# First-layer roots by way of device memory: a row of reciprocal roots goes over the partitions through a small array and two transfers, not through TensorE

## The chip, the cores and the metric

The kernel runs on one core of one Trainium2 chip. The metric is device time in microseconds of one execution. A core has TensorE (PE, matmuls; PEld its weight loads), VectorE (DVE), ScalarE (ACT), GpSimd (POOL) and SyncE (SP), each with its own instruction queue, worked in order, and 16 DMA engines that all of the queues share.

## The reference

Two layers over x (256 rows, 1024 columns, float32), then a last RMSNorm. One layer, cut to what matters:

```
def rms_norm(x, gain):
    xf = xf * lax.rsqrt(jnp.mean(xf * xf, axis=-1, keepdims=True) + EPS)
    return xf * gain

hn = rms_norm(x, norm_gain)
proj = jnp.einsum('bsd,de->bse', hn, w_in)
a_q, a_k, a_v, a_g, b_x, b_g, c_q, c_k, c_v, c_g = jnp.split(proj, ...)
y_a = dilated_attention(rope(a_q), rope(a_k), a_v) * silu(a_g)
y_b = rg_lru_branch(b_x, ...) * silu(b_g)
y_c = stick_breaking_attention(c_q, c_k, c_v) * silu(c_g)
return x + concat([y_a, y_b, y_c]) @ w_out
```

Only the factor `rsqrt(mean(x*x) + EPS)`, one number for each of the 256 rows of x, is touched by the change, and only in the first layer.

## The kernel before

Everything is in one program, `trunk_kernel`. Weights come as chunks of 128 x 2048 float32 (`w_pack`, two transfers of 512 KB each, issued by SyncE into five staging buffers `st`). To keep float32 accuracy each chunk is split in two: ScalarE rounds a quarter of it to the matmul's format (`whi`, line 109), VectorE subtracts that from the original (`wlo`, line 110), four of each a chunk. A product is then three matmuls: high by high, high by low, low by high (`mm3`, line 212). A staging buffer is free for the next transfer when VectorE has subtracted its second half.

**First layer.** Here the projections start from x itself (already transposed and multiplied by the gain, lines 142 to 171), without the normalising factor. Because that factor is one number for each row of x, it can be multiplied in later, on the results. `rms_stats` (line 191) makes it for each of the two blocks of 128 rows: ScalarE squares and sums, VectorE adds (line 196), ScalarE takes the logarithm and an exponential (`rstd`, lines 198 and 200). The result is a column: 128 partitions, one number each.

Results with rows of x on the partitions (`va`, `vc`, lines 385 and 386) take that column directly. Results that are kept transposed (heads on the partitions, rows of x along the free dimension) need the same 256 numbers as a row, repeated on all 128 partitions: the tile `rb`, 128 x 256. `rows_of_rstd` (line 373) makes it: VectorE scales the identity matrix by the column (line 377), TensorE multiplies a matrix of ones with it (line 378; a float32 matmul runs as two passes here, four in all), VectorE copies the result out of PSUM (line 379).

`rb` is then read by VectorE alone: in `scaled` (line 391) for `qc` and `kc`, the queries and keys of stick-breaking attention, and later for `bxp` and the gates; for `rp0`, the rotation tables multiplied by it (line 612); and in `rotated` (line 490).

**Order of the work.** TensorE's order is the order in which the program is written (a manual schedule for this engine). Around the change it is: chunk CQ (two halves of 128 outputs), chunk CK first half, `rows_of_rstd` (given to `proj_b` as `mid`, run between the two halves), CK second half, chunk AQ0 first half, the stick-breaking scores (line 442, which read `qc` and `kc`), AQ0 second half, AK0, BX and so on. On the other engines the framework's scheduler sets the order when the program is built; on the chip each engine then works through its list strictly. GpSimd has little to do: a polynomial of 4 columns, some memsets, and two transfers within SBUF, `xs` (line 565).

Of the kernel before, what the change touches and what calls it, by code (L numbers as in the profile page):

```python
# [9 lines left out]
F32 = mybir.dt.float32  # L10
# [3 lines left out]
ALU = mybir.AluOpType  # L14

P = 128
S = 256
D = 1024
L = 2
NT = S // P  # L20
# [22 lines left out]
CH_AV, CH_CV, CH_CQ, CH_CK, CH_BX, CH_CG, CH_BG, CH_AG, CH_O = 0, 2, 3, 4, 7, 10, 11, 12, 14  # L43
# [5 lines left out]
def trunk_kernel(ctx: ExitStack, tc: tile.TileContext, x, first_x, first, wpack, prm_d, gatew, gains, consts, rope, out):  # L49
    nc = tc.nc  # L50
    act, dve, pe, gps = nc.scalar, nc.vector, nc.tensor, nc.gpsimd

    cst = ctx.enter_context(tc.tile_pool(name="cst", bufs=1))
# [3 lines left out]
    wk = ctx.enter_context(tc.tile_pool(name="wk", bufs=2))  # L57
    pp = ctx.enter_context(tc.tile_pool(name="pp", bufs=3, space=bass.MemoryType.PSUM))
    at = ctx.enter_context(tc.tile_pool(name="at", bufs=4, space=bass.MemoryType.PSUM))
    yp = ctx.enter_context(tc.tile_pool(name="yp", bufs=1, space=bass.MemoryType.PSUM))  # L60

    def bank(pool, tag):
        return pool.tile([P, 512], F32, name=tag, tag=tag)

    def scr(w):
        return wk.tile([P, 512], F32, name="scr", tag="scr", bufs=SCR)[:, 0:w]
# [15 lines left out]
    def tab(*a, **k):  # L82
        i = dep(act.activation(*a, **k), loaded["load"])  # L83
        loaded["users"].append(i)
        return i

    def v2(a, n=2):
        return a.rearrange("p (b t) -> p b t", b=n)
# [28 lines left out]
    def ask(l, c, ahead=AHEAD):  # L117
        last = order.index((l, c)) + ahead
        while pending and order.index(pending[0]) <= last:
            i = pending.pop(0)  # L120
            ready[i] = load_chunk(*i)

    def weights(l, c, ahead=AHEAD):
        ask(l, c, ahead)
        return ready.pop((l, c))
# [16 lines left out]
    for k in range(NK):  # L142
# [7 lines left out]
        o = k % 2 * 768  # L150
# [16 lines left out]
        for (i, (a, b)), (ps, base, c0, c1) in seq:  # L167
            for t in range(NT):
                pe.matmul(ps[t][:, c0 - base:c1 - base], a[:, k, t * P:(t + 1) * P], b[:, c0:c1],  # L169
                          start=k == 0 and i == 0 and c0 == base, stop=k == NK - 1 and i == 2,  # L170
# [9 lines left out]
    ident = con[:, C_ID:C_ID + P]  # L180
# [4 lines left out]
    tiny_t = cst.tile([P, 48], F32, name="tiny")  # L185
    tiny = tiny_t[:, 0:1]
    dve.memset(tiny, 1e-19)
    ones = cst.tile([P, P], F32, name="ones")
    dve.memset(ones, 1.0)

    def rms_stats(t, eng):
        sq = wk.tile([P, 2], F32, name="sq", tag="sq", bufs=2)
        for i in range(2):
            act.activation(scr(512), xres[:, t, i * 512:(i + 1) * 512], AF.Square, accum_out=sq[:, i:i + 1])
        ss = wk.tile([P, 1], F32, name="ss", tag="ss", bufs=2)
        eng.tensor_scalar(ss, sq[:, 0:1], 1.0 / D, EPS, ALU.mult, ALU.add)
        ln = wk.tile([P, 1], F32, name="lnv", tag="lnv", bufs=2)
        tab(ln, sq[:, 1:2], AF.Ln, bias=ss, scale=1.0 / D)
        rstd = wk.tile([P, 1], F32, name="rstd", tag="rstd", bufs=4)
        tab(rstd, ln, AF.Exp, scale=-0.5)  # L200
        return rstd

# [4 lines left out]
    def mm3(ps, lhs, rhs, ks, first, last):  # L207
        lh, ll = lhs
        rh, rl = rhs
        seq = [(a, b, k) for a, b in ((lh, rh), (lh, rl), (ll, rh)) for k in ks]  # L210
        for i, (a, b, k) in enumerate(seq):
            pe.matmul(ps, a(k), b(k), start=first and i == 0, stop=last and i == len(seq) - 1)  # L212
# [33 lines left out]
    def normed(t):  # L246
        rstd = rms_stats(t, gps)
        xns = []
        for half in range(2):
            xn = scr(512)  # L250
            cs = slice(half * 512, half * 512 + 512)
            dve.scalar_tensor_tensor(xn, xres[:, t, cs], rstd, gn[:, cs], ALU.mult, ALU.mult)
            xns.append(xn)
        return xns
# [40 lines left out]
    rb = cst.tile([P, S], F32, name="rb")  # L295
    gn = cst.tile([P, D], F32, name="gn", tag="gn")

    for l in range(L):
# [14 lines left out]
        def proj_b(c, mid=None, to=None, sc=1.0):  # L313
            pair = c in PAIRED[l]
            hi, lo = [a.rearrange("p (k c) -> p k c", c=256) for a in weights(l, c, AHEAD - 1 if mid else AHEAD)]
            if pair:
                flat = None if to is not None else scr(512)
                to = [v2(flat)[:, b, :] for b in range(2)] if to is None else to
            else:
                flat = bank(pp, "pp")  # L320
            for b in range(2):
                cs = slice(b * P, b * P + P)
                if pair:
                    ps = bank(pp, "pp")
                    seq = [(0, k) for k in range(NK - 1)] + [(1, k) for k in range(NK)] + [(0, NK - 1)]
                    for i, (is_lo, k) in enumerate(seq):
                        if is_lo:
                            pe.matmul(ps[:, 0:S], lo[:, k, cs], xh[:, k, :], start=False, stop=False,  # L328
                                      skip_group_check=True)
                        else:  # L330
                            pe.matmul(ps, hi[:, k, cs], xx[:, k].rearrange("p h t -> p (h t)"), start=i == 0,  # L331
                                      stop=i == len(seq) - 1, skip_group_check=True)
                    low = wk.tile([P, S], F32, name="low", tag="low", bufs=2)
                    act.activation(low, ps[:, S:2 * S], AF.Copy, scale=sc)  # L334
                    if sc == 1.0:
                        dve.tensor_add(to[b], ps[:, 0:S], low)
                    else:
                        dve.scalar_tensor_tensor(to[b], ps[:, 0:S], sc, low, ALU.mult, ALU.add)
                else:
                    mm3(flat[:, b * 256:(b + 1) * 256], [lambda k, a=a: a[:, k, cs] for a in (hi, lo)],  # L340
                        [lambda k, a=a: a[:, k, :] for a in (xh, xl)], range(NK), True, True)
                if b == 0 and mid:
                    mid()
                    ask(l, c)
            return flat

        def proj_to(dst, c, mid=None, sc=1.0):
            if l > 0 and c in PAIRED[l]:
                proj_b(c, mid, [dst[:, b, :] for b in range(2)], sc)
            else:  # L350
                scaled(dst, proj_b(c, mid), sc)
# [16 lines left out]
            cv_bk = [cv_ps[:, t * 256:(t + 1) * 256] for t in range(NT)]  # L368

        if l == 0:  # L370
            rstd0 = [rms_stats(t, dve) for t in range(NT)]

        def rows_of_rstd():
            rb_ps = bank(yp, "y")
            for t in range(NT):
                dg = scr(P)
                dve.tensor_scalar(dg, ident, rstd0[t], None, ALU.mult)
                pe.matmul(rb_ps[:, t * P:(t + 1) * P], ones, dg, start=True, stop=True)
            dve.tensor_copy(rb, rb_ps[:, 0:S])

        va = sb.tile([P, NT, 512], F32, name="va", tag="va")
        vc = sb.tile([P, NT, 256], F32, name="vc", tag="vc")
# [5 lines left out]
        def scaled(dst, ps, sc=1.0):  # L388
            if l == 0:
                a, b = rows(ps)  # L390
                dve.scalar_tensor_tensor(dst, a, sc, b, ALU.mult, ALU.mult)
            else:
                act.activation(dst, v2(ps), AF.Copy, scale=sc)
# [208 lines left out]
        else:  # L602
            cq_ps = proj_b(CH_CQ)
        if l == 0:
            ck_ps = proj_b(CH_CK, rows_of_rstd)
            scaled(qc, cq_ps, 0.125)
            scaled(kc, ck_ps)
        else:
            proj_to(kc, CH_CK)
# [189 lines left out]
```

## Time and profile before

| | |
|---|---|
| median of 3 runs | 248.68 us (248.48 to 250.25) |
| the profiled execution's own time | 248.61 us |
| its span in the profile | 246.5 us |
| granted TensorE clock, mean | 0.995 |
| TensorE busy | 238.6 us |
| VectorE busy | 193.3 us |
| ScalarE busy | 170.5 us |
| GpSimd busy | 11.3 us |

The page of the profile gives busy time for each engine, the chain of work that ended last, and groups of instructions by line. Times of the timeline are microseconds from the span's start; a row has start, duration, engine, line, operation, `out<-in`, shape, count, and in brackets how long the engine was idle before it and what ended that. Consecutive instructions of one kind are one row.

### The profile page before, as it was taken

What the parts mean: (1) busy time and instruction counts of PE and PEld (TensorE: products, weight loads), DVE (VectorE), ACT (ScalarE), POOL (GpSimd) and SP (SyncE); (2) the same over time, 40 slices, a digit from 0 to 9 for tenths busy, and PEclk for the clock granted to TensorE, in tenths of its full rate; (3) what the DMA queues carried; (4) which work ended last, traced back from release to release, by engine and by line L of the source; (5) the groups of instructions that cost most, each with busy time, mean ns of one, the idle gap of its engine ahead of it and who ended that gap; (6) DMA issues with size and microseconds to landing.
All of it is one profiled execution on the core that took longest, in us unless ns stands there. A gap on an engine that the chain in (4) does not pass through costs nothing.

```text
span 246.5 us, 4741 instructions
## 1 busy us (share of the span) xinstructions
PE 238.6 (97%) x1753; PEld 212.4 (86%) x1753; DVE 193.3 (78%) x454; ACT 170.5 (69%) x368; POOL 11.3 (5%) x45
## 2 busy tenths in 40 slices
PE   7999999999999999999999999999999999999990
PEld 4889999999998899878889988888889889987870
DVE  3875599999999789986693666999999967985253
ACT  3867989854688499974672775876589749992142
POOL 0027100000100000000000000000010000000000
PEclk9999999999999999999999999999999999999997
DMA  6999799377737632277258387506462752000022
GB/s 208 390 289 412 313 316 322 112 237 255 229 102 233 231 96 78 89 237 251 108 166 256 101 297 256 201 6 204 148 205 56 233 228 85 3 0 0 3 85 85
DMA packets 13174, 43.90 MB, mean 178 GB/s; under 512 B 1632, under 2 KB 2144, under 8 KB 13152
## 3 DMA queue, kind: packets, MB, share of 16 engines
q1 hardware_dynamic: 12384, 42.30, 50.9%
q10 hardware_dynamic: 576, 0.79, 0.9%
q0 software_dynamic: 192, 0.52, 0.8%
q8 instruction: 14, 0.23, 0.3%
q14 instruction: 8, 0.07, 0.1%
HBM read 42.03 MB, written 1.05 MB: 175 GB/s over the span
## 4 chain that ended last, share of the span: by engine, by line
PE 94%; DMA 2%; DVE 1%; ACT 1%; SPq 0%; issue 0%; ACTq 0%
PE pp L212 51%; PE pp L331 11%; PE s L212 9%; PE pp L328 5%; PE s L169 4%; PE s L462 3%; PE s L514 2%; PE y L426 2%; DMA st<-first 2%; PE pp L169 2%; PE s L442 1%; PE pp L426 1%; PE s L573 1%; PE s L260 1%; DVE xres L689 0%; ACT scr L243 0%
## 5 line engine op out<-in xcount | busy, mean ns | idle before, releaser
L110 DVE TENSOR_TENSOR wlo<-st,whi 128x512 fp32r<-128x512 f32 x132 | 84.0, 684 | 12.6 <-ACT whi L109 12.3
L109 ACT ACTIVATE whi<-st 128x512 fp32r<-128x512 f32 x132 | 73.8, 628 | 20.2 <-DMA st<-w_pack 7.5
L212 PE MATMUL pp<-xx,whi 128*128 128x256 f32 x480 | 63.8, 285 | 0.0
L212 PEld LDWEIGHTS pp<-xx,whi 128*128 128x128 f32 x480 | 59.7, 191 | 1.3 <-ACT whi L109 0.4
L212 PE MATMUL pp<-xx,wlo 128*128 128x256 f32 x240 | 33.7, 283 | 0.0
L212 PEld LDWEIGHTS pp<-xx,wlo 128*128 128x128 f32 x240 | 31.0, 192 | 0.0
L331 PE MATMUL pp<-xx,whi 128*128 128x512 f32 x112 | 29.2, 396 | 0.0
L331 PEld LDWEIGHTS pp<-xx,whi 128*128 128x128 f32 x112 | 20.1, 189 | 3.9 <-ACT scr L83 0.3
L83 ACT ACTIVATE pr<-scr,mn 128x128 f32<-128x128 f32 (+1 forms) x32 | 14.1, 442 | 8.4 <-DVE mn L521 8.4
L77 ACT ACT_TABLE_LOAD x13 | 16.7, 1283 | 1.9 <-PEq L792 1.7
L328 PEld LDWEIGHTS pp<-xx,wlo 128*128 128x128 f32 x112 | 15.3, 190 | 1.1
L328 PE MATMUL pp<-xx,wlo 128*128 128x256 f32 x112 | 15.6, 282 | 0.0
L212 PE MATMUL pp<-whi,yh 128*128 128x512 f32 x48 | 14.4, 400 | 0.0
L212 PE MATMUL pp<-wlo,yh 128*128 128x512 f32 x48 | 13.8, 390 | 0.0
L212 PE MATMUL pp<-whi,yl 128*128 128x512 f32 x48 | 13.8, 389 | 0.0
L212 PEld LDWEIGHTS pp<-wlo,yh 128*128 128x128 f32 x48 | 9.0, 188 | 1.9
L212 PEld LDWEIGHTS pp<-whi,yl 128*128 128x128 f32 x48 | 9.0, 188 | 1.9
L212 PEld LDWEIGHTS pp<-whi,yh 128*128 128x128 f32 x48 | 8.6, 188 | 1.9 <-issue 0.3
L414 ACT ACTIVATE yh<-scr 128x512 fp32r<-128x512 f32 x8 | 5.1, 631 | 7.3 <-DVE scr L412 7.2
L169 PE MATMUL s<-whi,xx 128*128 128x512 f32 (+1 forms) x36 | 9.6, 384 | 0.2
L521 DVE CUSTOM_DVE_ANT_0 scr<-s,con 128x128 f32<-128x128 f32 (+1 forms) x32 | 9.2, 351 | 0.0
L334 ACT ACTIVATE low<-pp 128x256 f32<-128x256 f32 x14 | 5.3, 376 | 5.1 <-PE pp L331 5.1
(175 smaller groups left out, 357.4 us busy)
## 6 DMA issues: line engine op xcount, KB each, us to landing
st<-w_pack SPq DMA_DIRECT2D x66, 512.0 KB, 5.0
st<-first SPq DMA_DIRECT2D x7, 512.0 KB, 5.7
xres<-x_in SPq DMA_DIRECT2D x2, 512.0 KB, 8.7
gw_t<-gate_w SPq DMA_DIRECT2D x2, 256.0 KB, 7.7
gn<-gains SPq DMA_DIRECT2D x1, 512.0 KB, 6.2
xs<-xc POOLq DMA_DIRECT2D x4, 128.0 KB, 4.8
gf<-gains SPq DMA_DIRECT2D x1, 512.0 KB, 6.8
out<-scr SPq DMA_DIRECT2D x2, 256.0 KB, 2.1
```

What stands on the lines that cost most here:

```text
L77: load = act.preload_act_table_set(name)
L83: i = dep(act.activation(*a, **k), loaded["load"])
L109: split[l, c] = act.activation(hi[:, ws], st[:, ss], AF.Copy)
L110: dve.tensor_sub(lo[:, ws], st[:, ss], hi[:, ws].bitcast(F32))
L169: pe.matmul(ps[t][:, c0 - base:c1 - base], a[:, k, t * P:(t + 1) * P], b[:, c0:c1], start=k == 0 and i == 0 and c0 == base, stop=k == NK - ...
L212: pe.matmul(ps, a(k), b(k), start=first and i == 0, stop=last and i == len(seq) - 1)
L328: pe.matmul(ps[:, 0:S], lo[:, k, cs], xh[:, k, :], start=False, stop=False, skip_group_check=True)
L331: pe.matmul(ps, hi[:, k, cs], xx[:, k].rearrange("p h t -> p (h t)"), start=i == 0, stop=i == len(seq) - 1, skip_group_check=True)
L334: act.activation(low, ps[:, S:2 * S], AF.Copy, scale=sc)
L426: pe.matmul(y[hr, p * 128 + o:p * 128 + 256], vt[:, s0, hs], wts[i][s0], start=s0 == 0, stop=s0 == 1)
L462: pe.transpose(tp[:, i * P:(i + 1) * P], tiles[h0 + h][:, j * P:(j + 1) * P], ident)
L521: dve.tensor_tensor_reduce(xs[:, cs], sps[h][:, cs], nmask[:, cs], -0.125, 3e38, ALU.add, ALU.min, mn[:, t:t + 1])
```

## The change

`rms_stats` may now write its result into a given column. The two columns of the first layer lie side by side in a spare part of the tile `tiny` (`both`, 128 x 2). ScalarE issues a transfer that stores them, transposed, into an array `rd` of 2 x 128 float32 in device memory; GpSimd issues a transfer that loads these 256 numbers as one row, repeated, into all 128 partitions of `rb`. `rows_of_rstd`, its two scalings, its matmuls, its copy and the matrix of ones are gone, and `proj_b(CH_CK)` has no `mid` any more.

```
+    dr = ctx.enter_context(tc.tile_pool(name="dr", bufs=1, space=bass.MemoryType.DRAM))
...
-    ones = cst.tile([P, P], F32, name="ones")
-    dve.memset(ones, 1.0)
-
-    def rms_stats(t, eng):
+    def rms_stats(t, eng, rstd=None):
...
-        rstd = wk.tile([P, 1], F32, name="rstd", tag="rstd", bufs=4)
+        rstd = wk.tile([P, 1], F32, name="rstd", tag="rstd", bufs=4) if rstd is None else rstd
...
-            rstd0 = [rms_stats(t, dve) for t in range(NT)]
-
-        def rows_of_rstd():
-            rb_ps = bank(yp, "y")
-            for t in range(NT):
-                dg = scr(P)
-                dve.tensor_scalar(dg, ident, rstd0[t], None, ALU.mult)
-                pe.matmul(rb_ps[:, t * P:(t + 1) * P], ones, dg, start=True, stop=True)
-            dve.tensor_copy(rb, rb_ps[:, 0:S])
+            both = tiny_t[:, 32:32 + NT]
+            rstd0 = [rms_stats(t, dve, both[:, t:t + 1]) for t in range(NT)]
+            rd = dr.tile([NT, P], F32, name="rd")
+            act.dma_start(out=rd.rearrange("t p -> p t"), in_=both)
+            gps.dma_start(out=rb, in_=rd.rearrange("(o t) p -> o (t p)", o=1).broadcast_to([P, S]))
...
-            ck_ps = proj_b(CH_CK, rows_of_rstd)
+            ck_ps = proj_b(CH_CK)
```

Because VectorE's and ScalarE's lists are made by the scheduler, the change moves more than it names. The number behind a tile's name is its buffer; names in brackets are what the row waits for. VectorE before, from the last subtraction of chunk CK (`wlo_374`) through AQ0 (`wlo_388`) and AK0 (`wlo_484`) to `kc` (the two scalings of the identity stand some rows ahead of this piece):

```order
L110 TENSOR_TENSOR wlo_374<-st_381,whi_373 128x512 [waits Activation_49]
L110 TENSOR_TENSOR wlo_388<-st_389,whi_387 128x512 [waits DVE_49,DMAHW5_49,PE_49,Activation_49]
L110 TENSOR_TENSOR wlo_388<-st_389,whi_387 128x512 [waits Activation_49]
L110 TENSOR_TENSOR wlo_388<-st_395,whi_387 128x512 [waits DMAHW6_49,Activation_49]
L110 TENSOR_TENSOR wlo_388<-st_395,whi_387 128x512 [waits Activation_49]
L379 COPY rb_293<-y_475 128x256 [waits PE_49]
L110 TENSOR_TENSOR wlo_484<-st_485,whi_483 128x512 [waits DMAHW7_49,DVE_49,Activation_49]
L110 TENSOR_TENSOR wlo_484<-st_485,whi_483 128x512 [waits Activation_49]
L391 SCALAR_TENSOR_TENSOR qc_326<-pp_401,rb_293 128x512 [waits DVE_49]
L110 TENSOR_TENSOR wlo_484<-st_491,whi_483 128x512 [waits DMAHW0_49,Activation_49]
L110 TENSOR_TENSOR wlo_484<-st_491,whi_483 128x512 [waits Activation_49]
L391 SCALAR_TENSOR_TENSOR kc_327<-pp_450,rb_293 128x512 [waits PE_49]
```

VectorE after the change, the same place, from the last subtraction of CK (`wlo_375`) through AQ0 (`wlo_389`) to the first half of AK0 (`wlo_452`) and `kc`:

```order
L111 TENSOR_TENSOR wlo_375<-st_382,whi_374 128x512 [waits Activation_49]
L386 SCALAR_TENSOR_TENSOR qc_327<-pp_402,rb_293 128x512 [waits DMASW0_49,PE_49]
L111 TENSOR_TENSOR wlo_389<-st_390,whi_388 128x512 [waits DMAHW6_49,DVE_49,Activation_49]
L111 TENSOR_TENSOR wlo_389<-st_390,whi_388 128x512 [waits Activation_49]
L607 TENSOR_TENSOR rp0_292<-rp_291,rb_293 128x256 [waits DMAHW1_49]
L111 TENSOR_TENSOR wlo_389<-st_396,whi_388 128x512 [waits DMAHW7_49,Activation_49]
L111 TENSOR_TENSOR wlo_389<-st_396,whi_388 128x512 [waits Activation_49]
L607 TENSOR_TENSOR rp0_292<-rp_291,rb_293 128x256
L111 TENSOR_TENSOR wlo_452<-st_453,whi_451 128x512 [waits DMAHW0_49,DVE_49,Activation_49]
L111 TENSOR_TENSOR wlo_452<-st_453,whi_451 128x512 [waits Activation_49]
L386 SCALAR_TENSOR_TENSOR kc_328<-pp_465,rb_293 128x512 [waits PE_49]
```

`qc` moved ahead of the four subtractions of AQ0 and now waits for a transfer (`DMASW0`); the AQ0 subtractions and both halves of `rp0` stand between `qc` and `kc`; the second half of AK0's subtractions comes after `kc`.

ScalarE after the change, from the second root (written into `tiny`) to the first roundings of CK; before, the same rows stood there without the transfer:

```order
L84 ACTIVATE tiny_287<-lnv_312 128x1 [waits Activation_49]
L373 DMA rd_315<-tiny_287 128x2x1 [waits Activation_49]
L380 ACTIVATE va_318<-s_94,tiny_287 128x512
L381 ACTIVATE vc_319<-pp_96,tiny_287 128x256 [waits PE_49]
L110 ACTIVATE whi_374<-st_376 128x512 [waits DMAHW3_49]
L110 ACTIVATE whi_374<-st_376 128x512
```

The issue of the store is new in ScalarE's list, between the second root and `va`. On GpSimd the load of `rb` stands behind the polynomial and ahead of the memsets of the second layer and of the `xs` transfers; on TensorE only the four passes of line 378 are gone.

## The prediction

> **What bounds the kernel now.** I read the page first: span, busy shares and the chain that ended last.
>
> ```profile
> span 246.5 us, 4741 instructions
> PE 238.6 (97%) x1753; PEld 212.4 (86%) x1753; DVE 193.3 (78%) x454; ACT 170.5 (69%) x368; POOL 11.3 (5%) x45
> PE 94%; DMA 2%; DVE 1%; ACT 1%; SPq 0%; issue 0%; ACTq 0%
> ```
>
> TensorE is busy 97% of the span and is 94% of the chain: whatever makes it wait is added to the end almost in full, and whatever is taken off it comes off. Next I asked for busy time in the stretch of the first layer's projections.
>
> ```profile
> 32.00:38.00 6.00, 6.00 (x52) 5.87 (x52) 6.00 (x13) 5.23 (x9) 0.00 (x0) 1.00 0.93 325
> ```
>
> After the length come PE, PEld, DVE, ACT and POOL. PE has no idle time here, but VectorE has none either. So the question is not what the broadcast costs PE, but what VectorE has to do between the arrival of rb and the next point at which PE needs a result of it. That is in the timeline:
>
> ```profile
> 25.89 0.19 ACT L83 ACTIVATE rstd<-lnv 128x1 f32<-128x1 f32 x1
> 27.06 6.98 ACT L109 ACTIVATE whi<-st 128x512 fp32r<-128x512 f32 x12
> 27.72 4.90 DVE L110 TENSOR_TENSOR wlo<-st,whi 128x512 fp32r<-128x512 f32 x8 [1.31 <-ACT whi L109]
> 28.08 2.67 PE L212 MATMUL pp<-xx,whi 128*128 128x256 f32 x16
> 31.55 0.60 PE L378 MATMUL y<-scr,ones 128*128 128x128 f32 x4
> 31.91 2.16 PE L212 MATMUL pp<-xx,whi 128*128 128x256 f32 x16
> 32.54 0.41 DVE L379 COPY rb<-y 128x256 f32<-128x256 f32 x1
> 34.08 0.68 DVE L391 SCALAR_TENSOR_TENSOR qc<-pp,rb 128x512 f32<-128x512 f32 x1
> 34.68 1.28 DVE L110 TENSOR_TENSOR wlo<-st,whi 128x512 fp32r<-128x512 f32 x2
> 35.88 0.68 DVE L391 SCALAR_TENSOR_TENSOR kc<-pp,rb 128x512 f32<-128x512 f32 x1
> 36.48 0.75 DVE L612 TENSOR_TENSOR rp<-rp,rb 128x256 f32<-128x256 f32 x2
> 36.79 1.12 PE L212 MATMUL pp<-xx,wlo 128*128 128x256 f32 x8
> 37.15 1.89 DVE L110 TENSOR_TENSOR wlo<-st,whi 128x512 fp32r<-128x512 f32 x3
> 37.84 1.58 PE L442 MATMUL s<-kc,qc 64*128 64x128 f32 x16
> ```
>
> The second root is there at 25.89 + 0.19 = 26.08. The rows rb are complete at 32.95, VectorE scales qc and kc with them, kc is done at 36.56, and PE starts the stick-breaking scores (L442), which read qc and kc, at 37.84 without having waited: the matmuls before them (36.79 + 1.12 = 37.91) end into them. The present way has 37.84 - 36.56 = 1.28 us in hand.
>
> **What is removed.** Four PE passes of L378: from 31.55 to the next matmul at 31.91 the stream advances 0.36 us, and the chain in order of time has
>
> ```profile
> 31.71 0.44 PE y L378 x4
> ```
>
> I take 0.4. VectorE loses two scalings and the 0.41 copy; they lie beside PE's work, so nothing of that reaches the end.
>
> **What is added on ScalarE.** One DMA issue between the second root and va. The nearest rows are ScalarE's issues of a load at the start and of an output store at the end.
>
> ```profile
> 0.74 0.42 ACTq L132 DMA_DIRECT2D st<-first  x1
> 237.62 0.35 ACTq L244 DMA_DIRECT2D out<-scr  x1
> ```
>
> It takes 0.35 to 0.42 and pushes va, vc and the twelve whi back. The first four of these set PE's pace: sixteen matmuls at 28.08 took 2.67, where the same sixteen at 31.91 took 2.16. So the issue reaches PE with about 0.4, between 0 and 0.5. Removal and issue cancel: without any wait for rb, the scores would start at 37.84 again, to within some 0.1.
>
> **What is added as a wait.** rb now arrives at a time R, after a store of 256 pieces of 4 bytes and a load of 128 rows of 1 KB. Their prices, from the DMA issues (the last figure is us to landing), the xs tile's answer and the busy time by single us (the last two columns are the DMA engines' share and GB/s):
>
> ```profile
> 10.69 0.43 SPq L174 DMA_DIRECT2D prm_t<-prm  x1
> prm_t<-prm SPq DMA_DIRECT2D x1, 16.0 KB, 4.5
> 23.48 0.33 SPq L106 DMA_DIRECT2D st<-w_pack  x1
> st<-w_pack SPq DMA_DIRECT2D x1, 512.0 KB, 8.2
> out<-scr ACTq DMA_DIRECT2D x2, 256.0 KB, 2.4
> xs<-xc POOLq DMA_DIRECT2D x4, 128.0 KB, 4.8
> DMA to landing us min/median/max: 4.3/4.8/5.1
> 26.00:27.00 1.00, 1.00 (x10) 1.00 (x9) 0.29 (x1) 0.97 (x3) 0.00 (x0) 1.00 1.03 422
> 27.00:28.00 1.00, 1.00 (x11) 1.00 (x10) 0.28 (x1) 1.00 (x3) 0.00 (x0) 1.00 0.97 397
> 28.00:29.00 1.00, 0.98 (x8) 0.78 (x7) 1.00 (x3) 1.00 (x3) 0.00 (x0) 1.00 0.70 287
> 29.00:30.00 1.00, 0.98 (x8) 0.78 (x8) 1.00 (x3) 1.00 (x3) 0.00 (x0) 1.00 0.19 78
> ```
>
> *The store.* Below, ScalarE's store at the end of the kernel, with the DMA engines almost idle: 2.4. Above, the weight load issued at 23.48, behind others in SyncE's queue: 8.2. In between, the parameter load (rows of 128 bytes, issued at 10.69 into busy engines): 4.5. Our store is issued at 26.1, when the engines are at 1.03 and 0.97 of their time; only after 29 do they empty (0.19). It is on ScalarE's own queue, so it doesn't stand behind all of SyncE's loads, but each of its pieces shares an engine with them. Nearest is the 4.5 row; I take 4.0, for the way is free after 29. *The load.* POOL's only other transfers are the xs, same bytes, same queue, beside weight loads: 4.3 to 5.1. I take 4.8; nothing else is issued on POOL at this time, and its order puts the xs behind. With 0.1 between the two, R = 26.1 + 4.0 + 0.1 + 4.8 = 35.0. Bounds: 26.1 + 2.4 + 0.1 + 4.3 = 32.9 and 26.1 + 8.2 + 0.1 + 5.1 = 39.5.
>
> The Trainium skill, page "DMA: Bandwidth & Descriptors", section "Anatomy of one DMA — SWDGE (gpsimd) path", gives a fit of 2.0 us plus bytes over 436 GB/s per DMA. By it the pair would be an estimated 2.0 + 2.3, and R = 30.5. The same page, "Rules for kernel authors", says that a strided last dimension becomes one descriptor per element, which speaks for a store of 256 small pieces. The xs rows (4.3 to 5.1 for the size that the fit puts at 2.3) stand against the fit here.
>
> **What lies between R and the scores.** VectorE runs in order. In the changed program qc stands right behind the four subtractions of the CK chunk, which end near 30.6 (27.72 + 0.4 + four times 0.6). It waits there, and behind it wait, in this order: two subtractions of AQ0, half of rp0, two of AQ0, the other half of rp0, two of AK0, kc. Before, eight subtractions ran ahead of rb and two between qc and kc. So the stall takes with it work that had been done during the wait for rb. From the start-to-start times above: qc 0.60 (34.08 to 34.68), six subtractions at 0.60 (34.68 to 35.88 for two), two halves of rp0 at 0.335 (36.48 to 37.15), kc 0.68: 0.60 + 3.60 + 0.67 + 0.68 = 5.55, and 0.05 to PE. The scores start at R + 5.6 = 40.6, that is 40.6 - 37.84 = 2.8 us late. PE breaks even at R = 37.84 - 5.6 = 32.2. PE's own low matmuls of AQ0 need their last subtraction (R + 0.60 + 2.40 + 0.34 = 38.3) near 37.6; that smaller wait lies within the larger one.
>
> **What is late next.** PE's stream after the scores is 2.8 later as a whole. VectorE starts the scans after kc and five more subtractions, at R + 5.55 + 3.0 = 43.6 where it was 39.31: 4.3 late, 1.5 more than PE. These rows show that it has room for that:
>
> ```profile
> 39.31 1.31 DVE L453 TENSOR_TENSOR_SCAN sw<-scr,con 128x127 f32<-128x127 f32 x3 [0.28 <-ACT scr L83]
> 44.90 0.55 DVE L455 TENSOR_TENSOR sw<-scr,sw 128x384 f32<-128x384 f32 x1
> 48.09 2.08 PE L212 MATMUL pp<-xx,whi 128*128 128x256 f32 x16
> 50.97 0.60 PE L462 MATMUL s<-con,sw 128*128 128x128 f32 x4
> 36.01 2.33 ACT L109 ACTIVATE whi<-st 128x512 fp32r<-128x512 f32 x4 [0.67 <-DMA st<-w_pack]
> ```
>
> The last sw ended at 45.45, PE turned it from 50.97: 5.5 us spare. SyncE's loads wait for staging buffers that the late subtractions free, so from the fourth on they go out some 4 us late; but the BX weights were converted at 36.01 for matmuls at 48.09. None of this adds to the end, and none of it gives anything back, since PE has no idle time up to the last stage. Sum: 248.61 (the profiled execution) + 2.8 = 251.4; from the median 248.68, 251.5, which I forecast.
>
> **Rivals.** *Hidden.* Both transfers are quick and R is at most 33.2, so the scores start at most 1.0 late. For it: the 2.4 of the idle store, and an engine share of 0.19 at 29 to 30. Against it: the full engines when the store is issued, and that no POOL transfer landed under 4.3. At 32.2 and below it decides for no loss: 248.68 - 0.4 + 0.4, so 248.2 to 248.8; up to R = 33.2 it is 249.7 at most. The skill's fit would be this case. *Slow store.* The 256 pieces take turns with weight packets and the store takes nearer to 8.2: R = 36.5 to 39.5, scores 4.3 to 7.3 late, 253.0 to 256.0, say 254.5. For it: a load issued 2.6 us earlier needed 8.2. Against: it stood behind its own queue. *Slow PE after the gap.* PE ran slower at its start:
>
> ```profile
> 1.19 3.17 PE L140 MATMUL y<-cold 128*128 128x512 bf16 x7 [1.19 <-DVE cold L128]
> 230.41 0.62 PE L212 MATMUL s<-whi,yh 128*128 128x512 f32 x2
> 230.87 0.62 PE L212 MATMUL s<-wlo,yh 128*128 128x512 f32 x2
> ```
>
> Seven matmuls of 512 columns took 3.17 there (0.43 apart), later two advance 0.46 (0.23 apart). If the gap before the scores put PE back to that rate for another 3.2 us, it would lose 3.2 x (1 - 0.23/0.43) = 1.5: 251.5 + 1.5 = 253.0 or more. Against it: at R = 35.0 the longest gap is about 2 us (from some 38.6 to 40.6), and the granted clock is 1.00 in all rows above. The Trainium skill, "TensorE: Matmul & The Clock Gate", Part 1, has the clock halve after an idle window of some 3.4 us; by that it would need R near 36.5 or more.
>
> **How the numbers follow.** Forecast (R of 33.2 to 36.5, 249.7 to 253.0): 0.70. Hidden: 0.13. Slow store: 0.11. Slow PE: 0.06. A measurement tells about 1% (2.5 us) from no change, and that line is at R = 34.7, inside the forecast: I put 0.43 of its 0.70 above. Slower: 0.43 + 0.11 + 0.06 = 0.60. Faster by 1% would need more than is removed: 0.02. The same: 0.38. The range leaves out a tenth on either side: 249.3 (R = 32.9, the lower bound) to 254.7 (R = 38.2, most of the way to the upper).
>
> **What would show it.** Right: a VectorE idle stretch of some 4 us ended by the load of rb, just ahead of qc, near 35; kc done near 40.5; a PE wait of 2 to 3 us before L437 (the old L442) released by kc; DMA rows for rd near 4 and rb near 4.8; the rest of the timeline shifted by a constant; whi of CK 0.4 later. Wrong: no such VectorE idle time; scores at 38; a PE wait elsewhere, or a later stage longer than before.

## The result, and the profile after

| | before | after |
|---|---|---|
| median | 248.58 us (247.0 to 250.25, 6 runs) | 260.98 us (260.57 to 263.26, 6 runs) |
| ratio to before | | 1.0507 [1.0473, 1.0541] |
| span of the profiled execution | 246.5 us | 258.9 us |
| mean granted clock of that execution | 0.995 | 0.966 |

The changed kernel is 12.4 us slower, in the median and in the span; 251.5 was forecast, with a range to 254.7. One execution further down (255.55 us, in the last experiment) is a slow one and stays out of its kernel's median and ratio. The page of the changed kernel, with the lines that answer to those of before (slices of PEclk are 6.5 us each):

```profile
span 258.9 us, 4725 instructions
PE 242.2 (94%) x1749; PEld 214.6 (83%) x1749; DVE 192.3 (74%) x450; ACT 170.5 (66%) x368; POOL 12.3 (5%) x46
PEclk9999995589999999999999999999999999999996
PE 79%; DMA 12%; DVE 3%; ACT 2%; issue 2%; SPq 1%; DVEq 0%; ACTq 0%
```

DMA has gone from 2% to 12% of the chain that ended last, and the clock is down in two slices near 45 us. The timeline around the change, and the two transfers' rows among the DMA issues (the last figure is us to landing):

```profile
26.32 0.39 ACTq L373 DMA_DIRECT2D rd<-tiny  x1
28.36 2.50 DVE L111 TENSOR_TENSOR wlo<-st,whi 128x512 fp32r<-128x512 f32 x4 [3.80 <-ACT whi L110]
35.81 0.74 POOL L374 DMA_DIRECT2D rb<-rd  x1 [10.32 <-DMA rd<-tiny]
39.57 1.15 ACT L110 ACTIVATE whi<-st 128x512 fp32r<-128x512 f32 x2 [3.44 <-DMA st<-w_pack]
43.06 0.69 DVE L386 SCALAR_TENSOR_TENSOR qc<-pp,rb 128x512 f32<-128x512 f32 x1 [12.19 <-DMA rb<-rd]
44.40 2.94 PE L211 MATMUL pp<-xx,wlo 128*128 128x256 f32 x8 [7.24 <-DVE wlo L111]
47.94 0.69 DVE L386 SCALAR_TENSOR_TENSOR kc<-pp,rb 128x512 f32<-128x512 f32 x1
48.68 2.94 PE L437 MATMUL s<-kc,qc 64*128 64x128 f32 x16 [1.35 <-DVE kc L386]
```

```profile
rd<-tiny ACTq DMA_DIRECT2D x1, 1.0 KB, 9.2
rb<-rd POOLq DMA_DIRECT2D x1, 128.0 KB, 7.1
```

The store lands 9.2 us after its issue, the load takes 7.1, VectorE stands before `qc` for 12.19 us, and TensorE waits 7.24 us for the low weights of AQ0, whose subtractions stand behind `qc`. The scores begin at 48.68, where they began at 37.84: 10.84 late. From `qc` to the scores it is 5.62 us; 5.6 was forecast.

The DMA engines between 30 and 36 us, by the busy time of that stretch, before and after. The last two columns are the engines' share and GB/s:

```profile
30.00:36.00 6.00, 6.00 (x53) 6.00 (x52) 6.00 (x12) 5.04 (x8) 0.00 (x0) 1.00 0.89 296
```

```profile
30.00:36.00 6.00, 6.00 (x50) 6.00 (x51) 0.86 (x2) 3.09 (x6) 0.19 (x1) 1.00 1.09 32
```

The engines count as busy in both, but after the change they move 32 GB/s, not 296. That is 192 KB of weights in 6 us, under half of one 512 KB load, beside a store of 1 KB. The same rows for the time behind it (PEclk is the third figure from the end):

```profile
36.43:39.84 3.41, 0.73 (x7) 0.52 (x5) 0.00 (x0) 0.27 (x1) 0.12 (x1) 1.00 0.74 214
39.84:53.49 13.65, 7.60 (x33) 5.99 (x34) 10.43 (x20) 7.06 (x15) 0.00 (x0) 0.50 0.57 173
53.49:58.00 4.51, 4.51 (x39) 4.51 (x39) 4.51 (x12) 4.29 (x10) 0.00 (x0) 1.00 0.69 244
```

From 39.84 to 53.49 TensorE has half its clock.

### The profile page after: what moved, and what is told of

Read it like the earlier page. It is cut to its first block, busy times and chain, and to the rows that moved or that the text cites. A ratio compares the mean times of both kernels' runs of the same rounds, so it can differ in the third digit from the quotient of the medians.

```text
span 258.9 us, 4725 instructions
## 1 busy us (share of the span) xinstructions
PE 242.2 (94%) x1749; PEld 214.6 (83%) x1749; DVE 192.3 (74%) x450; ACT 170.5 (66%) x368; POOL 12.3 (5%) x46
## 4 chain that ended last, share of the span: by engine, by line
PE 79%; DMA 12%; DVE 3%; ACT 2%; issue 2%; SPq 1%; DVEq 0%; ACTq 0%
PE pp L211 43%; PE pp L330 10%; PE s L211 8%; PE pp L327 5%; DMA rd<-tiny 4%; DMA xres<-x_in 3%; PE s L457 3%; DMA rb<-rd 3%; DMA st<-first 2%; PE y L421 2%; PE s L509 2%; PE s L437 2%; DVE wlo L111 1%; PE pp L421 1%; PE s L568 1%
## 5 line engine op out<-in xcount | busy, mean ns | idle before, releaser
L211 PE MATMUL pp<-xx,whi 128*128 128x256 f32 x480 | 64.9, 288 | 0.1
L211 PEld LDWEIGHTS pp<-xx,whi 128*128 128x128 f32 x480 | 60.6, 194 | 2.1 <-ACT whi L110 1.0
L211 PE MATMUL pp<-xx,wlo 128*128 128x256 f32 x240 | 35.3, 290 | 7.4 <-DVE wlo L111 7.2
L211 PEld LDWEIGHTS pp<-xx,wlo 128*128 128x128 f32 x240 | 31.9, 196 | 8.1 <-DVE wlo L111 7.9
L330 PEld LDWEIGHTS pp<-xx,whi 128*128 128x128 f32 x112 | 20.1, 189 | 3.9 <-ACT scr L84 0.3
L327 PEld LDWEIGHTS pp<-xx,wlo 128*128 128x128 f32 x112 | 15.3, 190 | 1.1
L327 PE MATMUL pp<-xx,wlo 128*128 128x256 f32 x112 | 15.6, 282 | 0.0
L386 DVE SCALAR_TENSOR_TENSOR qc<-pp,rb 128x512 f32<-128x512 f32 x1 | 0.7, 692 | 12.2 <-DMA rb<-rd 12.2
```

## The experiments

Two explanations were open once the result was known. The theory: the store of 256 four-byte pieces is slow in itself and holds the DMA engines, so `rb` and the weights both come late. The rival: a store at this place takes 8 to 9 us whatever its pieces, because it stands among the weight loads. All medians below stand against the kernel before, run on the same chip at the same time; where there is one run only, its time and span are given.

### The transfers without the wait

The kernel before, with both transfers added and nobody waiting for them:

```
+            both = tiny_t[:, 32:32 + NT]
+            rstd0 = [rms_stats(t, dve, both[:, t:t + 1]) for t in range(NT)]
+            rd = dr.tile([NT, P], F32, name="rd")
+            spare = sb.tile([P, S], F32, name="spare", tag="it")
+            act.dma_start(out=rd.rearrange("t p -> p t"), in_=both)
+            gps.dma_start(out=spare, in_=rd.rearrange("(o t) p -> o (t p)", o=1).broadcast_to([P, S]))
```

> The kernel before, rb by TensorE, plus the store of 256 pieces and the load of its row into a tile that nobody reads. It has the transfers without the wait for them. Theory (the store holds the DMA engines): store near 9 us, the loads of AK0 and BX issued near 30 land near 39 to 41 as in the changed kernel; VectorE's list has two subtractions of AK0 between qc and kc, so kc comes near 42 and the scores 4 us late: 252 to 255, ratio 1.015 to 1.025. Rival (only the wait for rb costs, transfers beside it are harmless): 248.6 to 249.1, ratio 1.000 to 1.002.

Measured: 255.19 us (254.61 to 256.06), ratio 1.0295 [1.0256, 1.0335], a little over what was expected; the span of the profiled execution is 254.2.

```profile
rd<-tiny ACTq DMA_DIRECT2D x1, 1.0 KB, 10.1
40.47 1.15 ACT L111 ACTIVATE whi<-st 128x512 fp32r<-128x512 f32 x2 [3.26 <-DMA st<-w_pack]
43.08 2.93 PE L449 MATMUL s<-kc,qc 64*128 64x128 f32 x16 [4.69 <-DVE kc L398]
```

With nobody waiting for the broadcast, the scores are still 5.24 us late: ScalarE waits for weights (3.26 at 40.47, more before), VectorE's list goes late with it, and TensorE waits 4.69 for `kc`. So 7.0 us are lost without any wait for `rb`.

### One piece instead of 256

The changed kernel, but the store is a ready-made row of 1 KB from one partition; turning the column into a row is left out:

```
-            act.dma_start(out=rd.rearrange("t p -> p t"), in_=both)
+            act.dma_start(out=rd.rearrange("(o t) p -> o (t p)", o=1), in_=rp0[0:1, 0, :])
```

> The changed kernel, but the store moves one row of 1 KB that lies in one partition (ones and two roots, so the numbers in rb are not the roots; the turning of the column is left out) instead of 256 pieces of 4 bytes; same issue, same wait, same load behind it. Theory (small pieces to device memory hold the DMA engines): the store lands in 2.5 to 3.5 us instead of 9.2, weight loads between 30 and 38 us run at their old rate, rb lands in about 4.8 instead of 7.1, R near 34.5, scores near R + 5.6 = 40, clock stays 1.00, time near 251, ratio 1.01. Rival (the store stands behind the weight loads whatever its pieces are): it lands in 8 to 9 us again, R near 42, time near 260, ratio 1.045.

Measured: 252.82 us (252.3 to 253.29), ratio 1.0195 [1.0154, 1.0236], span 250.0.

```profile
24.98 0.49 ACTq L374 DMA_DIRECT2D rd<-rp  x1
29.37 0.74 POOL L375 DMA_DIRECT2D rb<-rd  x1 [3.98 <-DMA rd<-rp]
34.68 0.69 DVE L387 SCALAR_TENSOR_TENSOR qc<-pp,rb 128x512 f32<-128x512 f32 x1 [5.06 <-DMA rb<-rd]
40.31 1.93 PE L438 MATMUL s<-kc,qc 64*128 64x128 f32 x16 [1.63 <-DVE kc L387]
rb<-rd POOLq DMA_DIRECT2D x1, 128.0 KB, 5.2
```

From the issue of the store to POOL's issue of the load it is 4.39 us (24.98 to 29.37), where the changed kernel needs 9.49 (26.32 to 35.81). The load takes 5.2, not 7.1, `qc` runs at 34.68 and the scores at 40.31. That both lie so near the forecast (35.0 and 40.6) is in part luck: in this execution the second root was ready early and the store went out 1.3 us sooner than in the changed kernel, and store and load each took 0.4 more than was forecast. Because of this earlier issue the run alone does not settle the rival. The store in eight pieces further down does: issued at 26.24, as in the changed kernel, it is followed by the load after 3.69 us. The place is not what costs 9 us.

### The store alone, packed and spread

Four kernels add only a store to the kernel before, and one a transfer within the chip. They differ in the distance between the places to which the pieces go:

```
 packed     rd [NT, P]        pieces 4 bytes apart
 spread     rd [NT, P, 128]   act.dma_start(out=rd[:, :, 0:1]...)   512 bytes apart
            rd [NT, P, 16]    64 bytes apart
            rd [NT, P, 8]     32 bytes apart
 on chip    spare [P, 4]      act.dma_start(out=spare[:, 0:4:2], in_=both)
```

> The kernel before, with the store of the 256 four-byte roots alone added behind the second root; no load back, and nobody reads it. Theory (the store's small writes hold the DMA engines and with them the weight loads): the store takes 9 to 10 us, the scores begin 4 to 5 us late, and the time is 6 to 7 us over the kernel before, as with the store and the load together. Rival (the 128 KB load back is what crowds the weight loads): the scores are at most 1 us late, and the time within 1 us of before.

> As the store alone, but each four-byte piece goes to a place of its own 512 bytes from the next in device memory. If the slowness comes from neighbouring pieces that share a short stretch of device memory: the store takes 3 to 4 us and the scores are not late. If it is a matter of many small writes to device memory as such: 9 to 10 us and scores 4 to 5 us late, as the store alone.

> As the store alone, but the 256 four-byte pieces go from the column in the on-chip buffer to another tile in the on-chip buffer, each to its own partition. If writing to device memory is what holds the engines: about 3 us for the transfer, scores not late, the time within 1 us of before. If the number of four-byte pieces is what does it, wherever they go: 9 to 10 us and 6 to 7 us lost.

> As the store spread at 512 bytes, but the four-byte pieces lie 64 bytes apart in device memory, eight of them in each 512 bytes. If it is enough that no two pieces fall into the same 64 bytes: the store lands in 5 to 6 us and the scores are less than 1 us late, as at 512 bytes. If pieces that share 512 bytes hold one another up, as the packed ones do: 8 us or more and scores over 3 us late.

> As the store spread at 64 bytes, with 32 bytes between the four-byte pieces, so that two of them share each 64 bytes. If pieces in one 64-byte stretch hold one another up only in so far as they share it: a store a little over 5.6 us, 6 to 7, and scores at most 1 us late. If any sharing already brings the whole loss: 9 us and scores 4 to 5 us late. If 32 bytes are stretch enough: 5.6 us and no loss, as at 64 bytes.

| pieces | store to landing | scores begin | span | time, one run |
|---|---|---|---|---|
| packed, 4 bytes apart | 9.5 us | 42.76 | 252.4 | 254.48 |
| 32 bytes apart | 5.9 us | 37.56 | 245.9 | 248.02 |
| 64 bytes apart | 5.6 us | 37.51 | 245.7 | 247.81 |
| 512 bytes apart | 5.5 us | 38.37 | 247.6 | 249.70 |
| on-chip buffer | 5.6 us | 38.84 | 246.9 | 249.12 |

A store of 3 to 4 us had been expected for the pieces that are far apart or stay on the chip; all took 5.5 to 5.9. The moment of the issue differs between these runs: the second root came early where the pieces lie 32 and 64 bytes apart (issues at 25.40 and 25.34) and later in the other three (26.14 packed, 26.21 at 512 bytes, 26.40 on the chip). So the fair partner of the packed store is the one at 512 bytes, issued 0.07 us after it: 5.5 us, and 237 GB/s from 30 to 36. With the later issue ScalarE's roundings of CK come late too, and TensorE waits for them at 28 to 31 us; that is why the scores of the last two rows are 0.5 and 1.0 late although TensorE does not wait for `kc`. Their times lie 1.6 and 1.0 us over the median of the kernel before on that chip (248.07).

The row of the DMA issues and the stretch of 30 to 36 us, first of the packed store, then of the store spread at 32 bytes:

```profile
rd<-tiny ACTq DMA_DIRECT2D x1, 1.0 KB, 9.5
30.00:36.00 6.00, 6.00 (x52) 6.00 (x52) 3.51 (x7) 2.45 (x6) 0.00 (x0) 1.00 1.08 29
42.76 2.26 PE L447 MATMUL s<-kc,qc 64*128 64x128 f32 x16 [4.38 <-DVE kc L396]
```

```profile
rd<-tiny ACTq DMA_DIRECT2D x1, 1.0 KB, 5.9
30.00:36.00 6.00, 6.00 (x52) 6.00 (x52) 6.00 (x11) 4.80 (x9) 0.00 (x0) 1.00 0.95 275
37.56 1.58 PE L447 MATMUL s<-kc,qc 64*128 64x128 f32 x16
```

The number, the size and the target of the pieces are the same in both; what differs is their distance, and by 0.74 us the moment of the issue, which the store at 512 bytes rules out as the cause. Packed, the engines move 29 GB/s and the loss is there, with no load back and no reader. At 32 bytes they move 275 GB/s and nothing is lost. So what holds the engines is that the small writes go to neighbouring places in device memory; 32 bytes from one to the next are enough to be rid of it. Distances between 4 and 32 were not tried, and what the memory does with such neighbours no run shows. My expectations had left open which distance would be enough.

The Trainium skill, "DMA: Bandwidth & Descriptors", section "Specifications", says that transfers under 512 bytes are done by reading, changing and writing back. If that took whole stretches of 512 bytes here, eight pieces 64 bytes apart would have held one another up; they did not (5.6 us, 282 GB/s in the same stretch of time). The rule does not tell the bad case from the good one here, since all five are of 4 bytes; the distance does.

### VectorE's order

The changed kernel, with the subtractions of AQ0 and AK0 put ahead of `qc`, `kc` and `rp0` on VectorE by dependences that carry order only:

```
-            scaled(qc, cq_ps, 0.125)
-            scaled(kc, ck_ps)
+            dep(scaled(qc, cq_ps, 0.125), subs[0, CH_AK[0]])
+            kc_in = dep(scaled(kc, ck_ps), subs[0, CH_AK[0]])
...
-                dve.tensor_mul(rp0[:, i, :], rp[:, i, :], rb)
+                dep(dve.tensor_mul(rp0[:, i, :], rp[:, i, :], rb), kc_in)
```

> The changed kernel with VectorE's list in another order: all eight subtractions of AQ0 and AK0 ahead of qc, kc right behind it, then rp0. Theory (the scores start at R plus what stands between rb and kc on VectorE): with qc and kc alone between, 1.3 us instead of 5.6; rb at 43.0 or a little later since the last AK0 weights came late too, scores near 45, about 3.5 us earlier than in the changed kernel; time near 257.5, ratio 1.036. Rival (R alone counts, the rest hides elsewhere or is taken back by late weights): time within 1 us of 261.

Measured: 257.61 us (257.01 to 258.15), ratio 1.039 [1.0353, 1.0426].

```profile
43.55 0.69 DVE L386 SCALAR_TENSOR_TENSOR qc<-pp,rb 128x512 f32<-128x512 f32 x1 [2.40 <-DMA rb<-rd]
44.16 0.68 DVE L386 SCALAR_TENSOR_TENSOR kc<-pp,rb 128x512 f32<-128x512 f32 x1
44.90 2.93 PE L437 MATMUL s<-kc,qc 64*128 64x128 f32 x16 [8.47 <-DVE kc L386]
```

The scores follow `qc` after 1.35 us, not 5.62. Those 4.3 us of the changed kernel's loss are VectorE's own work that its list has put behind the wait, as the prediction's sum has it. `rb` came 0.5 later here, so the scores gain 3.8 (44.90, not 48.68), and the median 3.4.

### The half clock

The changed kernel with matmuls that nobody reads, 29 of them ahead of AQ0's low matmuls, into a bank of their own:

```
+                        idle = bank(yp, "y")
+                        for i in range(FILL):
+                            pe.matmul(idle, hi[:, i % NK, cs], xx[:, i % NK].rearrange("p h t -> p (h t)"),
+                                      start=True, stop=True)
```

> The changed kernel with 29 extra matmuls (their result is never read) ahead of TensorE's low matmuls of AQ0, where TensorE stood idle for 7.2 us; 29 x 0.227 = 6.6 us, so they end before the wait does. Theory (half clock): the idle gap put the granted clock to 0.5 from 39.8 to 53.5 us, and this took the lateness of TensorE from 10.8 us at the scores (48.68 against 37.84) to 13.0 at 54.4; with the gap filled the clock stays at 1.00, the scores start at 48.7 again, and the kernel is about 2.2 us faster than the changed one: near 258.8, ratio to before near 1.041. Rival (the rest of the lateness is waiting on late weights, the clock only follows): clock 1.00, time unchanged at 261, ratio 1.05.

Measured: 261.04 us (260.06 to 261.75), ratio 1.0526 [1.0481, 1.057]: no gain, against the expectation. Then with 33 there, 2 more behind the fourth low block and 10 behind AK0's last:

> The changed kernel with 33 never-read filler matmuls ahead of AQ0's low matmuls, 2 more behind the fourth low block and 10 more behind the last one of AK0, so that TensorE also works in the wait for the key's columns. Theory (the half clock comes from TensorE standing still and costs about 2 of the 12.4 us): the granted clock stays at 1.00 from 38 to 55 us, the scores begin about 10.8 us late as in the changed kernel and nothing is added behind them, so the time is about 2 us under the changed kernel's, near 1.042 of the kernel before. Rival (the clock falls for another reason, or the lost time behind the scores is not the clock's): 1.05 again.

Measured: 259.42 us (258.86 to 260.2), ratio 1.0466 [1.0426, 1.0506]. First the kernel with 29, then the one with 45:

```profile
35.90 6.76 PE L346 MATMUL y<-xx,whi 128*128 128x512 f32 x29
41.75:45.16 3.41, 1.92 (x9) 1.00 (x7) 2.86 (x6) 0.79 (x2) 0.00 (x0) 1.00 0.01 2
45.16:51.99 6.83, 5.46 (x25) 4.24 (x26) 6.83 (x12) 2.52 (x5) 0.00 (x0) 0.50 0.86 283
```

```profile
38.00:54.00 16.00, 15.80 (x96) 12.76 (x96) 12.18 (x22) 8.27 (x15) 0.00 (x0) 1.00 0.64 191
47.99 1.58 PE L452 MATMUL s<-kc,qc 64*128 64x128 f32 x16
```

The 29 ended at 42.66; behind the shorter waits that were left the clock fell at 45.16. With 45 it stays at 1.00, the scores begin 10.15 late, and the span (257.0) is 10.5 over before: almost nothing is added behind the scores, where the changed kernel adds 12.4 - 10.84 = 1.6. The intervals of the two ratios overlap, so the rows show this, and the times alone do not; the ratio of 1.042 that I had expected was too low.

### The change with another store

A whole version: VectorE turns the two columns on the chip in blocks of 32 by 32, so that the store is 8 pieces of 128 bytes:

```
+            both = cst.tile([P, 64], F32, name="both")
+            flip = cst.tile([P, 64], F32, name="flip")
+            dve.memset(both, 0.0)
...
+            dve.transpose(flip, both)
+            act.dma_start(out=rd.rearrange("t (b c) -> b t c", b=4),
+                          in_=flip[0:P:32, :].rearrange("b (t c) -> b t c", t=NT))
```

> A whole version of the change with another store: VectorE turns the two columns in blocks of 32 by 32 on the chip, so that the store is 8 pieces of 128 bytes, not 256 of 4; the scheduler puts its issue behind the second va, about 0.9 us later than in the changed kernel. Theory (the 256 adjacent small writes are what cost the extra 8 us): the store lands in about 4, the load in about 5 us, rb is there near 36, the scores begin near 41.7, 3.8 us late, and with 1 to 2 us of half clock behind the gap the time is 4 to 6 us over before, 252 to 254. Rival (any store and load through device memory costs this at this place): store 9, scores 10 late, 258 or more.

The second kernel adds VectorE's order of the experiment above.

> The same store, and VectorE's order as in the late-qc kernel: the subtractions of AQ0 and AK0 stand ahead of qc, kc and the two halves of rp0. Theory: those subtractions end near 36 whatever rb does, rb arrives at about the same time, kc is done near 37.6 and the scores begin less than 0.5 us late; TensorE has no gap, the clock stays, and the time is within 1 us of the kernel before (ratio 0.998 to 1.004). Rival (the order on VectorE matters little and the wait for rb itself costs): 3 us or more over before.

Measured: the first 253.41 us (252.8 to 253.68), ratio 1.0213 [1.0179, 1.0247]. The second 251.39 (median of five runs, 250.43 to 252.91), ratio 1.0143 [1.0104, 1.0182], where 0.998 to 1.004 was expected. The first kernel's rows:

```profile
26.24 1.10 ACTq L376 DMA_DIRECT2D rd<-flip  x1
29.93 0.75 POOL L378 DMA_DIRECT2D rb<-rd  x1 [3.84 <-DMA rd<-flip]
35.09 0.69 DVE L390 SCALAR_TENSOR_TENSOR qc<-pp,rb 128x512 f32<-128x512 f32 x1 [4.18 <-DMA rb<-rd]
40.38 1.58 PE L441 MATMUL s<-kc,qc 64*128 64x128 f32 x16 [1.64 <-DVE kc L390]
43.58 1.32 DVE L452 TENSOR_TENSOR_SCAN sw<-scr,con 128x127 f32<-128x127 f32 x3
61.64 0.63 ACT L110 ACTIVATE whi<-st 128x512 fp32r<-128x512 f32 x1 [1.49 <-DMA st<-w_pack]
62.18 1.07 ACT L462 ACTIVATE wv<-s 128x512 f32<-128x512 f32 x2
62.81 0.99 PE L513 MATMUL s<-k,q 32*128 32x128 f32 x10 [1.67 <-ACT wv L462]
```

The store (3.69 us from its issue to that of the load) and the load (5.1) are near what was forecast for the change, `qc` runs at 35.09 and the scores at 40.38. The time lies in the expected 252 to 254, but in part by luck: the half clock that was to add 1 to 2 us behind the gap did not come. Instead this kernel loses another 1.67 us at 62.81. There, TensorE waits for ScalarE's copies `wv` (which free the banks of the next scores); these stand in ScalarE's list behind a `whi` that waits for a weight load; and that load waits for a staging buffer that VectorE's late subtractions free (issued at 57.08 behind a wait for `wlo`; before, at 52.81). This chain is read from the waits in the trace; no run takes it out. The same rows before the change, without a wait of TensorE:

```profile
57.05 0.63 ACT L109 ACTIVATE whi<-st 128x512 fp32r<-128x512 f32 x1 [1.05 <-DMA st<-w_pack]
57.59 1.06 ACT L463 ACTIVATE wv<-s 128x512 f32<-128x512 f32 x2
```

`wv` is 4.6 us late where the scores are 2.5 late. In the second kernel the scores are no longer the matter, but the same wait is there:

```profile
38.44 1.58 PE L441 MATMUL s<-kc,qc 64*128 64x128 f32 x16 [0.56 <-DVE kc L390]
60.15 1.06 ACT L462 ACTIVATE wv<-s 128x512 f32<-128x512 f32 x2
60.78 1.30 PE L513 MATMUL s<-k,q 32*128 32x128 f32 x10 [1.59 <-ACT wv L462]
```

These rows are of the execution of 255.55 us, which has 6.83 us of half clock behind this wait. The other five have no trace; four of them have spans of 247.7 to 248.5, about 2.2 over the median of the kernel before (245.7), which fits the 0.6 and the 1.6 of these rows. Its times lie 2.3 to 4.1 us over its spans, those of before 2.1 to 2.3; where that comes from stays open. Neither version beats the kernel before.

## Why the prediction was wrong

**The step that failed: the price of the store.** "Nearest is the 4.5 row; I take 4.0, for the way is free after 29." It measured 9.2, past the upper bound of 8.2. The load, priced at 4.8 with 5.1 as its bound, took 7.1. Of the 8.0 us by which `rb` came later than forecast (43.0, not 35.0), the store has 5.2, the load 2.3 (7.1, not 4.8), and the starts of the two issues the rest. The rows that I priced by were transfers of rows of 128 bytes and more. One had the right queue (2.4, with idle engines), another had busy engines (4.5, on SyncE's queue), but none had neighbouring four-byte writes, so the upper bound did not hold. With a store in one piece or in eight pieces the load could be issued 4.39 and 3.69 us after it, and the load took 5.2 and 5.1: some 2 us of the load's price go with the packed store too.

**The sum:** 2.8 forecast and 8.0 more from `rb` up to the scores, and 1.6 behind them, which makes the 12.4 measured. Where extra matmuls kept the clock at 1.00, 0.4 of the 1.6 was left.

**The store as a holder.** I asked how long the engines would hold up the store, not how long the store would hold up the engines. The rival *slow store* came nearest in size (scores 7.3 late at its upper end; 10.84 were measured), but it priced only the wait for `rb`, and its reason, pieces that take turns with weight packets, is not what the runs show: as many pieces took 5.5 to 5.9 beside the same weight loads once they lay apart. The weight loads that it held back cost 5.2 us at the scores with no wait for `rb` at all. In the changed kernel both delays run beside each other: VectorE stands before `qc` anyway while the weights are late, so they don't add up.

**Slow PE after the gap,** given 0.06, came about. The prediction joined it to a single gap that needed R near 36.5. R was 43.0, so it was due by that reckoning too; but it also came in the kernel with one piece, at a gap of 1.63 us, so the condition was too strict (last section). Its price of 1.5 is near the 1.6 behind the scores.

**What is late next.** "None of this adds to the end" does not hold in general. In the changed kernel TensorE itself was so late that VectorE's lateness stayed hidden; in the kernel with the better store it was not, and `wv` cost 1.67. I had followed the late loads to the conversion of BX and not to what stands behind a conversion in ScalarE's list.

**What held.** VectorE's idle time ended by the load, ahead of `qc`; the 5.6 from there to the scores (5.62; 5.63 with one piece); the 0.39 of ScalarE's issue; VectorE's scans near 43.6 for R = 35 (43.58 with the eight pieces). The Trainium skill's fit ("DMA: Bandwidth & Descriptors", "Anatomy of one DMA — SWDGE (gpsimd) path") is given for transfers that GpSimd issues, so the prediction could draw on it for the load (an estimated 2.3 us) but not for ScalarE's store. The load disagrees with it in every run: 5.1 at best, beside weight loads.

## What to carry to other kernels

A column that is turned into a row by a transfer is one write per element, and neighbouring elements in device memory then hold all DMA engines: here 1 KB brought the weight stream down to about a tenth for 6 us. Turn it on the chip first, or spread the pieces (32 bytes from one to the next was enough here for the store alone; a whole version, whose load would have to gather the spread pieces, was not run), and price a transfer by a row of the same pieces, not of the same bytes. When a wait moves into an engine's strict list, follow each instruction behind it to its reader, and each late buffer to what stands behind it in the next engine's list.

## What the runs showed of the hardware

**Adjacent small writes.** 256 four-byte writes to neighbouring addresses brought the 16 engines from 296 to 29 to 39 GB/s for 6 us (32 in the changed kernel, 39 with both transfers unused, 29 with the store alone); the same writes 32 bytes apart did not (275). Spread or on the chip, 256 pieces still took 5.5 to 5.9; after one piece or eight the load could be issued 4.39 and 3.69 us behind the store's issue.

**The granted clock goes by windows.** It was at one half for 3.41, 6.83, 10.24 or 13.65 us in these profiles, whole multiples of 3.41 (a stretch at the very end, which the end of the program cuts off, left out). So I divided the time into windows of 3.41 us that fit these changes (in the kernel with eight pieces, those at the program's start and end). First the window ahead of a fall and the one behind it in the kernel with one piece, then the same place in the kernel with eight, which has no fall, then a window without a fall behind it in the kernel with the packed store alone:

```profile
37.99:41.41 3.42, 1.69 (x17) 1.36 (x18) 3.42 (x8) 0.78 (x2) 0.00 (x0) 1.00 0.88 302
41.41:44.82 3.41, 3.41 (x18) 2.76 (x15) 3.41 (x8) 3.20 (x9) 0.00 (x0) 0.50 0.88 278
```

```profile
38.51:41.92 3.41, 1.77 (x19) 1.19 (x18) 3.41 (x8) 1.20 (x3) 0.00 (x0) 1.00 0.87 274
41.92:45.34 3.42, 3.42 (x31) 3.42 (x30) 3.42 (x8) 2.87 (x8) 0.00 (x0) 1.00 0.83 249
```

```profile
36.68:40.09 3.41, 1.70 (x15) 1.50 (x13) 1.33 (x3) 0.00 (x0) 0.00 (x0) 1.00 0.76 192
```

The first two kernels both waited 1.6 us for `kc`. TensorE was busy for 1.69 of 3.42 in the one and the clock fell; for 1.77 of 3.41 in the other and it stayed. In the packed store's kernel TensorE stood still for 4.38 us ahead of 42.76, and yet the clock stayed behind the window shown (1.70 of 3.41 busy) and fell only behind the next one (22% busy). So the length of one gap does not decide. It fell behind windows that were 0 to 34% busy, but near half these records draw no line: it fell at 49% and, in the kernel with 29 matmuls, at 56% (1.92 of 3.41), and it stayed at 50% and 52%. The Trainium skill, "TensorE: Matmul & The Clock Gate", Part 1, has windows of some 3.4 us that run freely, which agrees with the multiples; that the window must be an idle one does not, for these were half busy.
